# Attention scores of two heads made together, the low part of K in half the array's rows per head

## The chip, the core and the metric

The kernel runs on one core of one Trainium2 chip. The time is device microseconds (us) of one execution, from the first to the last instruction of the program with what the device needs around it. Before the change three runs took 1198.54, 1198.84 and 1199.20 us; the median is 1198.84 us.

## The reference, cut to what matters

Two layers, each with one mixer and no feed-forward. 512 latent tokens and 256 context tokens, 1024 wide. A layer normalises and modulates its input, projects it once into the queries, keys and values of three groups of heads (A, B, C, each with 8 heads of 64) and a gate, lets each group attend in its own way, multiplies by the gate, projects back and adds. The change touches group A only: global attention, 8 query heads over 2 key and value heads, so that four query heads share one K and V.

```python
def global_gqa(q, k, v, qc, kc, vc, cos, sin, qn, kn, need_ctx):
    q = apply_rope(rmsnorm(heads(q, N_HEADS_A), qn), cos, sin) * scale
    k = apply_rope(rmsnorm(heads(k, N_KV_A), kn), cos, sin)
    ...
    k_all = jnp.concatenate([k, kc], axis=1)        # 512 latent + 256 context keys
    v_all = jnp.concatenate([v, vc], axis=1)
    def block(qi):                                   # 128 queries
        s = jnp.einsum('bqhgd,bkhd->bhgqk', qi, k_all)
        p = softmax_f32(s, v_all.dtype)
        return jnp.einsum('bhgqk,bkhd->bqhgd', p, v_all)
```

## The kernel before, in words

Nearly all matmuls take operands of the type `F32R`. To keep precision each operand is split into a high part and the low rest (`hi` is x copied to `F32R`, `lo = x - hi`), and a product is made as several passes that add up in PSUM.

**Scores of group A.** A head has 64 numbers, the array 128 rows, and the kernel uses both halves. The stationary operand is a tile of Q for 128 queries: rows 0 to 63 hold the high part of q, rows 64 to 127 the low part (`a_pair`, L883 to L905, where `qd` is laid out and turned). K is held twice: `K[:, 0]` has its high part in both halves of the rows, `K[:, 1]` its low part in both halves. A pass over `K[:, 0]` so gives (q_hi + q_lo)·k_hi, and a pass over `K[:, 1]` adds (q_hi + q_lo)·k_lo. For 128 queries of one head there are four passes: 256 context keys and 512 latent keys, each over both parts of K (L1152). Every matmul in this kernel brings its own load of the stationary operand, also where the one before it used the same.

**Units.** A pair of heads is attended in units. For group A a `GlobalUnit` is one head and two tiles of 128 queries (`units`, L1308): two per head, four per pair of heads. With 4 pairs in each of 2 layers there are 32 such units. `scores()` makes the eight passes into `Sbig`, three PSUM banks of 512 numbers: tile 0 of the unit takes columns 0 to 767, tile 1 columns 768 to 1535. Then, for each tile, VectorE takes the negated maximum (`negm`, L1158) and ScalarE the exponential with its sum (`P`, L1160). `values()` turns P on TensorE (`T`, L1054), splits the turned block into `pth` (ScalarE, L798) and `ptl` (VectorE, L1044), and multiplies both with V into `Obig` (L1049). `o_out` (L1069) adds the two halves of the result: ScalarE copies 64x256 out, VectorE adds (L1072). In the first layer a `CtxUnit` per head follows for the 256 context queries. Groups B and C have units of their own, which the change leaves alone.

**Order.** The Python program writes attention and projections as generators. `weave` steps between the attention of one pair (`attend`) and the projections of a later one (`PLAN`, L33), by the costs that each `yield` names; `zipped` runs the scores of a unit beside the values of the one before. The list so written is a priority; a scheduler then puts the instructions of each engine in order, with `tc.high_priority` moving a piece ahead and `after` tying one instruction behind another on the same engine without a semaphore. The last stage of a layer projects back (`head`, `finish_result`).

**One place where the array is already cut.** The modulation vectors are made by `ada` (L203): eight matmuls with a stationary operand of two columns, in four groups of 32 columns of the array (`pm[32 * g:32 * g + 2]`, L214). They run in the 32-bit float format, where each matmul appears as two instructions, 16 in all per call.

Of the kernel before, what the change touches and what calls it, by code (L numbers as in the profile page):

```python
# [11 lines left out]
F32 = mybir.dt.float32  # L12
F32R = mybir.dt.float32r
BF16 = mybir.dt.bfloat16
AF = mybir.ActivationFunctionType
# [6 lines left out]
NT = 512  # L22
# [749 lines left out]
def mixers(tc, nc, l, last, p1, ps, const, env):  # L772
# [110 lines left out]
    def a_pair(i, bank):  # L883
# [3 lines left out]
        def done(p, t2):  # L887
# [160 lines left out]
    def mul(*args, **kw):  # L1048
        m = nc.tensor.matmul(*args, **kw)  # L1049
        pace["pe"] = m.ins.name  # L1050
        return m
# [17 lines left out]
    def o_out(O, OT, h, c0, n):  # L1069
        tmp = p1.tile([64, 512], F32, name="otmp", bufs=1)  # L1070
        nc.scalar.activation(tmp[:, 0:n], O[64:128, 0:n], AF.Copy)
        nc.vector.tensor_add(OT[64 * h:64 * h + 64, c0:c0 + n], O[0:64, 0:n], tmp[:, 0:n])  # L1072

    third = {"n": 2}

# [5 lines left out]
    class Unit:  # L1081
# [5 lines left out]

        def stat(self, name, i, n=1):
            if name not in self.c:
                self.c[name] = p1.tile([128, 12], F32, name=name, bufs=2)  # L1090
            return self.c[name][:, self.h * 6 + i:self.h * 6 + i + n]

# [51 lines left out]

    class GlobalUnit(Unit):
        def scores(self):
            self.P = []
            for i in self.tiles:
                cx, loc = ((512, 0), (768, 1024))[i % 2]
                for c0, c1, o in ((NT, NA, cx), (0, NT, loc)):  # L1150
                    for x in range(2):
                        mul(Sbig[:, o:o + c1 - c0], self.Q[:, i * 128:(i + 1) * 128],  # L1152
                                         self.K[:, x, c0:c1], start=(x == 0), stop=(x == 1), skip_group_check=True)
                yield 0.65
            for i in self.tiles:
                S = Sbig[:, 768 * (i % 2):768 * (i % 2) + 768]
                nm = self.stat("negm", i)
                nc.vector.tensor_reduce(nm, S, axis=AX.X, op=OP.max, negate=True)  # L1158
                P = newP()
                nc.scalar.activation(P, S, AF.Exp, bias=nm, accum_out=self.stat("sums", i))  # L1160
                self.P.append(P)
                yield 0

        def values(self):
            O = half_O()

            def turns(k2):
                T = psT()
                for k in range(2):
                    for j in range(2):  # L1170

                        o = ((k2 + k + 2) % 6 if j else k2 + k) * 128
                        turn(T[:, (2 * k + j) * 128:(2 * k + j + 1) * 128], self.P[j][:, o:o + 128], ident)
# [7 lines left out]
            o_out(O, self.OT(), self.h, self.tiles[0] * 128, 256)  # L1181

# [105 lines left out]
    def units(kind, i, Q, K, V, G, extra):  # L1288
        c = dict(kind=kind, i=i, Q=Q, G=G)
        out = []  # L1290
        for h in range(2):
            if kind == "B":
# [13 lines left out]
            v = lambda kb, vh=vh: V[:, kb, vh].rearrange("p x f -> p (x f)")  # L1306
            if kind == "A":
                out += [GlobalUnit(c, h, k, v, tiles=t) for t in ((0, 1), (2, 3))]  # L1308
            else:
                out.append((NearUnit if kind == "B" else BandUnit)(c, h, k, v, sink, bm))  # L1310
# [360 lines left out]
```

## Time and profile before

| | |
|---|---|
| Runs | 1198.54, 1198.84, 1199.20 us |
| Span of the profiled execution | 1197.7 us (1.1 us below the median run) |
| Busy: TensorE / weight loads / VectorE / ScalarE / GpSimd | 96% / 86% / 64% / 58% / 34% |
| Matmuls | 8016 |
| Granted TensorE clock, mean | 0.996 |
| Attention of group A within | 265 to 560 us (layer 0), 885 to 1112 us (layer 1) |

The page lists groups of instructions by line, engine and tile, with their busy time and the mean duration of one. A matmul's duration holds its way through the array and the end is modelled; what it costs a row of matmuls is the distance from its start to the next start. The timeline merges neighbours of one kind: "x8" with a start and a length, where the length runs to the end of the last one. PE is TensorE's matmuls, PEld its loads of the stationary operand, which run beside them. What follows an instruction in square brackets is the idle time of its engine ahead of it and what ended that; "issue" means that the engine waited for nothing that the profile shows.

### The profile page before, as it was taken

How to read it: one execution, taken by the hardware profiler on the slowest of the kernel's cores; microseconds unless marked ns; L12 is line 12 of the kernel's file. 1: busy time of each engine (PE TensorE's matmuls, PEld its weight loads, DVE VectorE, ACT ScalarE, POOL GpSimd, SP SyncE). 2: the span in 40 equal slices, each digit the busy share in tenths (PEclk: the TensorE clock that was granted, in tenths of full speed). 3: DMA queues.
4: the chain of work that ended last, by engine and by line, in shares of the span. 5: the costliest groups of instructions: out<-in, count | busy, mean ns of one | idle time of the engine just before them, and what ended most of it. 6: DMA issues, size and time to landing. Idle time of an engine off the chain costs nothing.

```text
span 1197.7 us, 21749 instructions
## 1 busy us (share of the span) xinstructions
PE 1150.5 (96%) x8016; PEld 1034.8 (86%) x8016; DVE 769.4 (64%) x1548; ACT 696.9 (58%) x1581; POOL 408.1 (34%) x496
## 2 busy tenths in 40 slices
PE   5999999999999999999999999999999999998997
PEld 3898999998898988988778999989988888887876
DVE  5767566764656665568578895567754556567563
ACT  5446555656666676588423544555666667677552
POOL 1341110234446354385000030202274563656001
PEclk9999999999999999999999999999999999999999
DMA  9552222313312112123086662323222111232152
GB/s 321 213 142 89 78 78 67 123 66 104 111 70 92 67 44 92 34 63 119 27 293 198 205 210 74 98 84 109 91 73 67 53 46 53 63 88 72 36 161 77
DMA packets 60826, 124.22 MB, mean 104 GB/s; under 512 B 7216, under 2 KB 13488, under 8 KB 60720
## 3 DMA queue, kind: packets, MB, share of 16 engines
q1 hardware_dynamic: 54768, 111.96, 29.6%
q10 hardware_dynamic: 5952, 10.88, 2.7%
q8 instruction: 63, 1.03, 0.3%
q14 instruction: 43, 0.35, 0.1%
HBM read 109.05 MB, written 11.14 MB: 100 GB/s over the span
## 4 chain that ended last, share of the span: by engine, by line
PE 81%; DVE 5%; ACT 5%; DMA 3%; issue 3%; POOL 1%; SPq 0%; ACTq 0%; DVEq 0%; POOLq 0%
PE pj L318 18%; PE pj L341 17%; PE Sbig L1049 9%; PE Obig L1049 9%; PE T L1054 9%; PE pj L519 5%; PE T L519 3%; PE Sbig L519 3%; PE T L341 2%; PE Sbig L430 2%; DVE ptl L1044 1%; DMA x<-xT_dram 1%; PE Sbig L341 1%; ACT pth L798 1%; PE pj L430 1%
## 5 line engine op out<-in xcount | busy, mean ns | idle before, releaser
L1044 DVE TENSOR_TENSOR ptl<-T,pth 128x512 fp32r<-128x512 f32 (+2 forms) x312 | 181.1, 591 | 128.6 <-ACT pth L798 126.7
L798 ACT ACTIVATE pth<-T 128x512 fp32r<-128x512 f32 (+2 forms) x312 | 158.9, 520 | 134.8 <-PE T L1054 128.1
L341 PE MATMUL pj<-wh,hL 128*128 128x256 f32 x896 | 180.6, 287 | 0.0
L318 PE MATMUL pj<-hL,wh 128*128 128x512 f32 x544 | 175.0, 401 | 0.9 <-ACT wh L247 0.5
L1054 PE MATMUL T<-ident,P 128*128 128x128 f32 x1024 | 165.7, 273 | 4.0 <-ACT qt L902 1.7
L247 ACT ACTIVATE wh<-ws 128x512 fp32r<-128x512 f32 x192 | 119.5, 629 | 78.6 <-PE pj L318 16.3
L1049 PE MATMUL Sbig<-kt,qt 128*128 128x256 f32 (+1 forms) x864 | 156.2, 308 | 4.6 <-ACT P L1160 2.5
L250 POOL TENSOR_TENSOR wl<-ws,wh 128x512 fp32r<-128x512 f32 x76 | 98.5, 1300 | 146.4 <-ACT wh L247 146.4
L341 PEld LDWEIGHTS pj<-wh,hL 128*128 128x128 f32 x896 | 144.2, 190 | 1.0 <-issue 0.2
L1049 PE MATMUL Obig<-pth,vt 128*128 128x256 f32 (+2 forms) x432 | 134.6, 321 | 4.6 <-ACT pth L798 2.0
L1054 PEld LDWEIGHTS T<-ident,P 128*128 128x128 f32 x1024 | 123.0, 140 | 17.6 <-DVE ptl L1044 2.2
L1049 PE MATMUL Obig<-ptl,vt 128*128 128x256 f32 (+2 forms) x432 | 131.4, 318 | 5.0 <-DVE ptl L1044 4.3
L1049 PEld LDWEIGHTS Sbig<-kt,qt 128*128 128x128 f32 x864 | 123.3, 189 | 13.4 <-DVE negm L1208 4.1
L341 PE MATMUL pj<-wl,hL 128*128 128x256 f32 x448 | 128.0, 286 | 0.0
L318 PEld LDWEIGHTS pj<-hL,wh 128*128 128x128 f32 x544 | 96.2, 189 | 16.7 <-ACT wh L247 0.9
L250 DVE TENSOR_TENSOR wl<-ws,wh 128x512 fp32r<-128x512 f32 x116 | 82.7, 720 | 40.4 <-ACT wh L247 31.6
L318 PE MATMUL pj<-hL,wl 128*128 128x512 f32 x272 | 107.1, 394 | 0.5 <-DVE wl L250 0.5
L1049 PEld LDWEIGHTS Obig<-pth,vt 128*128 128x128 f32 x432 | 81.6, 189 | 15.9 <-ACT pth L798 7.1
L1049 PEld LDWEIGHTS Obig<-ptl,vt 128*128 128x128 f32 x432 | 81.5, 189 | 14.7 <-DVE ptl L1044 11.3
L1445 POOL TENSOR_TENSOR bm<-wr,bm 128x192 f32<-128x192 f32 (+1 forms) x48 | 41.3, 888 | 139.6 <-DMA bm<-mskB_dram 132.4
L341 PEld LDWEIGHTS pj<-wl,hL 128*128 128x128 f32 x448 | 85.4, 191 | 0.3
L1158 DVE TENSOR_REDUCE negm<-Sbig 128x1 f32<-128x768 f32 x64 | 61.0, 953 | 29.7 <-PE Sbig L1049 15.7
(336 smaller groups left out, 2495.6 us busy)
## 6 DMA issues: line engine op xcount, KB each, us to landing
ws<-wf_dram SPq DMA_DIRECT2D x72, 256.0 KB, 3.1
ws<-wt_dram SPq DMA_DIRECT2D x72, 256.0 KB, 3.0
ada<-adaw_dram SPq DMA_DIRECT2D x32, 512.0 KB, 5.5
ws<-wo_dram SPq DMA_DIRECT2D x57, 256.0 KB, 2.8
bm<-mskB_dram SPq DMA_DIRECT2D x16, 576.0 KB, 3.7
dw<-adat_dram SPq DMA_DIRECT2D x8, 512.0 KB, 8.2
dots<-adat_dram SPq DMA_DIRECT2D x16, 256.0 KB, 4.5
u<-u ACTq DMA_DIRECT2D x9, 384.0 KB, 2.9
```

Of the source, the lines that this page charges most:

```text
L247: nc.scalar.activation(hi, src, AF.Copy)
L250: eng.tensor_sub(lo, src, hi.bitcast(F32))
L318: paced(nc.tensor.matmul(p[:, 0:n], a[:, r, :], cols(b[kt], c0, n), start=(i == 0), stop=(i == 23)), i)
L341: paced(nc.tensor.matmul(p[:, t * 256:(t + 1) * 256], tok(a[kt], t2 + t), b[:, r, :], start=(i == 0), stop=(i == 23)), i)
L430: mm = nc.tensor.matmul(out, a, b, start=begin, stop=(kt == KT - 1 and i == 2), skip_group_check=True)
L519: mm = nc.tensor.matmul(p[:, 0:n], a[:, r, :], ucols(ua[b][ft], c0, n), start=(ft == FT_ORDER[0] and i == 0), stop=(ft == FT_ORDER[-1] and ...
L798: nc.scalar.activation(out, src, AF.Copy)
L1044: i = nc.vector.tensor_sub(lo[:, 0:n], T[:, 0:n], hi[:, 0:n].bitcast(F32))
L1049: m = nc.tensor.matmul(*args, **kw)
L1054: m = nc.tensor.transpose(*args, **kw)
L1158: nc.vector.tensor_reduce(nm, S, axis=AX.X, op=OP.max, negate=True)
L1445: nc.gpsimd.tensor_add(b, src, b)
```

## The change

Three things are changed, all in group A.

1. **Unit.** A unit is now one tile of 128 queries and both heads of the pair (`tiles=(t,)`, four units per pair, as many as before). Head 0 has columns 0 to 767 of `Sbig`, head 1 columns 768 to 1535. The two context units of a pair come after its four global ones.
2. **Layout of Q.** Head 0 keeps high, low; head 1 is laid out low, high. The high part of head 0 is in rows 0 to 63, that of head 1 in rows 64 to 127.
3. **Passes.** Five whole passes as before: the high part of K for context and latent keys of both heads, and the low part for the context keys of head 0. The rest of the low part is done in five passes of 64 rows and 256 keys each: head 0 on rows 0 to 63, head 1 on rows 64 to 127, in turn, head 1 first. Their stationary operand is the high part of q alone, so q_lo·k_lo is no longer added there. Two neighbours in this row have different rows and different PSUM banks. The five are tied one behind the other and behind the whole passes, and raised in priority.

`o_both` takes the place of `o_out`: one copy of 64x256 on ScalarE as before, but two additions of 64x128 on VectorE, since the two heads go to different rows of `OT`. Copies and subtractions of Q are as many as before, with other strides.

```diff
-            nc.scalar.activation(qd[:, :, 0:64], t1, AF.Copy)
-            e.tensor_sub(qd[:, :, 64:128], t1, qd[:, :, 0:64].bitcast(F32))
+            blocks = qd.rearrange("p a f -> p (a f)").rearrange("p (t b f) -> p t b f", t=2, b=4)
+            hi, lo = blocks[:, :, 0:4:3], blocks[:, :, 1:3]
+            src = t1.rearrange("p (t h) f -> p t h f", t=2)
+            nc.scalar.activation(hi, src, AF.Copy)
+            e.tensor_sub(lo, src, hi.bitcast(F32))
...
+    def o_both(O, OT, c0):
+        tmp = p1.tile([64, 512], F32, name="otmp", bufs=1)
+        nc.scalar.activation(tmp[:, 0:256], O[64:128, 0:256], AF.Copy)
+        for h in range(2):
+            nc.vector.tensor_add(OT[64 * h:64 * h + 64, c0:c0 + 128], O[0:64, h * 128:h * 128 + 128],
+                                 tmp[:, h * 128:h * 128 + 128])
...
         def scores(self):
-            for i in self.tiles:
-                cx, loc = ((512, 0), (768, 1024))[i % 2]
-                for c0, c1, o in ((NT, NA, cx), (0, NT, loc)):
-                    for x in range(2):
-                        mul(Sbig[:, o:o + c1 - c0], self.Q[:, i * 128:(i + 1) * 128],
-                                         self.K[:, x, c0:c1], start=(x == 0), stop=(x == 1), skip_group_check=True)
-                yield 0.65
+            i = self.tiles[0]
+            Q = [q[:, i * 128:(i + 1) * 128] for q in self.c["Q"]]
+            whole = []
+            for h, x, c0, c1, o in ((0, 0, NT, NA, 512), (0, 1, NT, NA, 512), (1, 0, NT, NA, 768), (0, 0, 0, NT, 0),
+                                    (1, 0, 0, NT, 1024)):
+                whole.append(mul(Sbig[:, o:o + c1 - c0], Q[h], self.K[:, x, c0:c1], start=(x == 0 and o != 768),
+                                 stop=False, skip_group_check=True))
+                if o == 768:
+                    after(whole[2], whole[0].ins.name)
+                yield (c1 - c0) / 2400
+            last = None
+            for h, c0, o in ((1, NT, 768), (0, 0, 0), (1, 0, 1024), (0, 256, 256), (1, 256, 1280)):
+                r = slice(64 * h, 64 * h + 64)
+                with tc.high_priority(offset=200):
+                    m = mul(Sbig[:, o:o + 256], Q[h][r], self.K[r, 1, c0:c0 + 256], start=False, stop=True,
+                            skip_group_check=True)
+                for w in whole[1:] if last is None else (last,):
+                    after(m, w.ins.name)
+                last = m
+            yield 0.33
...
+        if kind == "A":
+            out += [GlobalUnit(c, 0, K[i // 2], v, tiles=(t,)) for t in range(4)]
...
-            if kind == "A":
-                out += [GlobalUnit(c, h, k, v, tiles=t) for t in ((0, 1), (2, 3))]
```

What this does to the order on TensorE, at the first unit of group A in layer 1. `Sbig` is written by the passes of the scores, `pj` by projections, `T` by turned blocks; L1049 of before is L1052 of the change. Before:

```order
3807 L899 MATMUL T<-identr,qd 128x128 x4
3808 L1049 MATMUL Obig<-pth,vt 128x2x128
3809 L1049 MATMUL Sbig<-kt,qt 128x256 x2
3810 L1049 MATMUL Sbig<-kt,qt 128x512 x2
3811 L1049 MATMUL Sbig<-kt,qt 128x256 x2
3812 L1049 MATMUL Sbig<-kt,qt 128x512 x2
3813 L318 MATMUL pj<-hC,wh 128x256 x2
```

The same place in the changed kernel:

```order
3804 L902 MATMUL T<-identr,qd 128x128 x4
3805 L1052 MATMUL Obig<-pth,vt 128x2x128
3806 L1052 MATMUL Sbig<-kt,qt 128x256 x3
3807 L1052 MATMUL Sbig<-kt,qt 128x512 x2
3808 L1052 MATMUL Sbig<-kt,qt 128x256 x5
3809 L318 MATMUL pj<-hL,wh 128x512 x2
```

Eight passes (four of 256 columns, four of 512) became three of 256, two of 512 and the five half-row passes, which stand in one row; this is so at all 32 units. Before, both passes of a score were neighbours and tile 0 was complete after half of the row; now the last pass of head 0 is the last but one of ten.

On VectorE, in the first pair of group A in layer 0, before (L1044 is `ptl`, L1158 the maximum, L1072 the addition of `o_out`, L1121 the maximum of a context unit):

```order
392 L1121 TENSOR_REDUCE negm<-Sbig 128x2
393 L1044 TENSOR_TENSOR ptl<-T,pth 128x512 x3
394 L1072 TENSOR_TENSOR OT<-Obig,otmp 64x256
395 L1158 TENSOR_REDUCE negm<-Sbig 128x1
396 L1044 TENSOR_TENSOR ptl<-T,pth 128x512
397 L1158 TENSOR_REDUCE negm<-Sbig 128x1
398 L1044 TENSOR_TENSOR ptl<-T,pth 128x512
399 L874 TENSOR_TENSOR vt<-T,vt 128x4x64 x2
400 L1072 TENSOR_TENSOR OT<-Obig,otmp 64x256
```

And in the changed kernel (L1047, L1185, L1082 and L1133 in the same roles):

```order
392 L1185 TENSOR_REDUCE negm<-Sbig 128x1
393 L1047 TENSOR_TENSOR ptl<-T,pth 128x512 x3
394 L1185 TENSOR_REDUCE negm<-Sbig 128x1
395 L1082 TENSOR_TENSOR OT<-Obig,otmp 64x128 x2
396 L1047 TENSOR_TENSOR ptl<-T,pth 128x512
397 L1185 TENSOR_REDUCE negm<-Sbig 128x1
398 L1047 TENSOR_TENSOR ptl<-T,pth 128x512
399 L874 TENSOR_TENSOR vt<-T,vt 128x4x64 x2
400 L1082 TENSOR_TENSOR OT<-Obig,otmp 64x128 x2
401 L1133 TENSOR_REDUCE negm<-Sbig 128x2
```

The addition is two instructions, and the context unit's maximum has moved behind the global units; the rest stands as it did.

More of the change, by code (lines that the diff above doesn't have):

```diff
@@ L1169, in turns @@
                 for k in range(2):
-                    for j in range(2):
-                        o = ((k2 + k + 2) % 6 if j else k2 + k) * 128
-                        turn(T[:, (2 * k + j) * 128:(2 * k + j + 1) * 128], self.P[j][:, o:o + 128], ident)
+                    for h in range(2):
+                        o = ((k2 + k + 2) % 6 if h else k2 + k) * 128
+                        turn(T[:, (2 * k + h) * 128:(2 * k + h + 1) * 128], self.P[h][:, o:o + 128], ident)
                 return pt_copy(T, 512)
@@ L1180, in values @@
             yield from ahead([(lambda k2=k2: turns(k2), lambda pt, k2=k2: sums(k2, pt), 0.45) for k2 in range(0, 6, 2)])
-            o_out(O, self.OT(), self.h, self.tiles[0] * 128, 256)
+            o_both(O, self.OT(), self.tiles[0] * 128)
     KS = [(0, 1), (0, 1, 2), (1, 2, 3), (2, 3)]
```

16 lines of the change are left out of this document (9 added, 7 removed).

## The prediction, made before the result was known

> **What bounds the kernel now.** I read the page first, then the timeline of TensorE (PE) and of its weight loads (PEld) around one unit of group A, then the one place where the array is already used in parts. The page's busy times, its chain and four of its groups:
>
> ```profile
> PE 1150.5 (96%) x8016; PEld 1034.8 (86%) x8016; DVE 769.4 (64%) x1548; ACT 696.9 (58%) x1581; POOL 408.1 (34%) x496
> PE 81%; DVE 5%; ACT 5%; DMA 3%; issue 3%; POOL 1%; SPq 0%; ACTq 0%; DVEq 0%; POOLq 0%
> L1054 PE MATMUL T<-ident,P 128*128 128x128 f32 x1024 | 165.7, 273 | 4.0 <-ACT qt L902 1.7
> L1049 PE MATMUL Sbig<-kt,qt 128*128 128x256 f32 (+1 forms) x864 | 156.2, 308 | 4.6 <-ACT P L1160 2.5
> L1158 DVE TENSOR_REDUCE negm<-Sbig 128x1 f32<-128x768 f32 x64 | 61.0, 953 | 29.7 <-PE Sbig L1049 15.7
> ```
>
> PE is busy for 96% of the span and makes 81% of the chain. The windows of group A (layer 0, then layer 1) show the same within the stages that the change touches:
>
> ```profile
> 265.00:560.00 295.00, 288.51 (x2130) 260.01 (x2129) 184.61 (x358) 195.19 (x453) 156.48 (x176) 1.00 0.25 80
> 885.00:1112.00 227.00, 216.23 (x1434) 191.50 (x1433) 136.29 (x247) 157.60 (x342) 126.05 (x139) 1.00 0.20 61
> ```
>
> The columns are length, then busy time of PE, PEld, VectorE (DVE), ScalarE and GpSimd. PE has 295.00 - 288.51 = 6.5 us idle in the first and 10.8 us in the second, at a full clock. So PE's time counts nearly one for one: what a unit gains or loses on PE, 32 times over, is the change in the end.
>
> **What a unit costs on PE now.** The eight passes of one unit, with the passes before and behind them:
>
> ```profile
> 385.64 0.40 PE L318 MATMUL pj<-hL,wl 128*128 128x512 f32 x1
> 385.87 1.56 PE L1049 MATMUL Sbig<-kt,qt 128*128 128x256 f32 x8
> 387.28 0.60 PE L1054 MATMUL T<-ident,P 128*128 128x128 f32 x4
> ```
>
> From 385.87 to 387.28 is 1.41 us for four passes of 256 columns and four of 512. A pass of 512 takes 385.87 - 385.64 = 0.23 from start to start; that leaves (1.41 - 4 x 0.23) / 4 = 0.12 for a pass of 256. The weight loads of these passes cost nothing of their own, since each runs under the pass before it:
>
> ```profile
> 385.64 1.36 PEld L1049 LDWEIGHTS Sbig<-kt,qt 128*128 128x128 f32 x8
> ```
>
> **What the change does to it.** Five whole passes stay: 3 x 0.12 + 2 x 0.23 = 0.82. One of 256 and two of 512 go, 0.12 + 2 x 0.23 = 0.58, and five passes of 64 rows and 256 keys take their place. If two of these run at a time they need three rounds, 3 x 0.12 = 0.36, provided nothing is lost at the border between whole and half passes. So 0.58 is the price to beat, and two questions decide: what the border costs, and whether the loads of two halves run together.
>
> **The border.** No row of before has a pass of 64 rows. The nearest thing is L214, where four matmuls share the array by columns. Its surroundings:
>
> ```profile
> 406.38 0.28 PE L341 MATMUL pj<-wl,hL 128*128 128x256 f32 x1
> 406.50 0.28 PE L341 MATMUL pj<-wh,hL 128*128 128x256 f32 x1
> 406.71 1.04 PE L214 MATMUL pj<-ada,silu_c 128*2 128x256 f32 x16
> 407.69 0.38 PE L1049 MATMUL Obig<-pth,vt 128*128 128x256 f32 x1
> 407.91 0.28 PE L1049 MATMUL Obig<-ptl,vt 128*128 128x256 f32 x1
> 408.03 0.28 PE L1049 MATMUL Obig<-pth,vt 128*128 128x256 f32 x1
> 408.26 0.60 PE L1054 MATMUL T<-ident,P 128*128 128x128 f32 x4
> L214 PE MATMUL pj<-ada,silu_c 128*2 128x256 f32 x128 | 8.4, 378 | 0.0
> ```
>
> Side by side works there: 16 passes last from 406.71 to the last start, 406.71 + 1.04 - 0.38 = 407.37, which is three rounds of four at 0.22 each. But the border has a price on both sides. Going in, the pass ahead (406.50) is followed after 0.21 instead of 0.12: 0.09 lost. Ordinary neighbours, 407.91 and 408.03, are 0.12 apart. Coming out, 407.69 - 407.37 = 0.32 instead of the 0.22 of a round: 0.10 lost. Then the first whole pass is followed after 407.91 - 407.69 = 0.22 instead of 0.12: its weight load had no pass to hide under, 0.10 lost. The loads tell that nothing else was waited for:
>
> ```profile
> 279.09 0.54 PEld L214 LDWEIGHTS pj<-ada,silu_c 128*2 128x2 f32 x16 [0.25 <-issue]
> 280.06 0.19 PEld L1049 LDWEIGHTS Obig<-pth,vt 128*128 128x128 f32 x1 [0.44 <-issue]
> ...
> 488.14 0.19 PEld L1049 LDWEIGHTS Obig<-pth,vt 128*128 128x128 f32 x1 [0.44 <-issue]
> ```
>
> All three idle times end by "issue", and behind two blocks 200 us apart it is the same 0.44. I read this as the array running empty when the way it is cut changes, with the next load held until then. The Trainium skill says the same on the page "TensorEngine Tiling (Array Packing)", section "Tiling Modes", under its key properties: a change of the tiling mode, not of the tile, drains TensorE; the trace agrees, with 0.09 going in and 0.10 coming out, and the page gives no price.
>
> For half passes one more term comes in. The loads of L214 have two columns; those of the change have 128. A load of 128 columns takes 0.11: the four turned blocks at 408.26 are bound by theirs, and start (0.60 - 0.27) / 3 = 0.11 apart, with 0.273 as the length of one from the page. Behind a drained array the first of them is bare. The skill's page "TensorE: Matmul & The Clock Gate", section "LDWEIGHTS (loading the stationary operand)", says that a load's time goes by its columns, not its rows, by which half the rows save nothing; its figure, 128 / 1.2, is an estimate of 107 ns and agrees with the 0.11.
>
> **The sum for one unit, as I forecast it.** In 0.09, first load 0.11, three rounds 0.36, out 0.10, first whole load 0.10: 0.76. Against 0.58 that is +0.18 us. The ends are 0.36 (no border at all, below zero by 0.22) and 1.00 (loads one at a time: five rounds instead of three, +0.24 on 0.76). I take 0.76 because L214 is the only row in which the array is cut, and it shows both a price and side by side. 32 units x 0.18 = +5.8 us.
>
> No semaphore is added: the half passes follow the whole ones by their place in PE's queue, and what is queued behind them (projections, mostly) waits for the 0.18 and nothing else.
>
> **The rest of the change.**
>
> ```profile
> L1072 DVE TENSOR_TENSOR OT<-Obig,otmp 64x256 f32<-64x256 f32 x56 | 23.2, 414 | 23.9 <-ACT otmp L1071 23.4
> L1072 DVE TENSOR_TENSOR OT<-Obig,otmp 64x512 f32<-64x512 f32 x32 | 21.8, 682 | 12.9 <-ACT otmp L1071 12.4
> PE Obig L1049 <- DVE OT L1072: 0.3, 1, 0.3
> PE Obig L1049 <- DVE OT L1072: 1.3, 2, 0.7
> PE Sbig L1049 <- ACT P L1160: 1.8, 2, 1.1
> PE Sbig L1049 <- ACT P L1160: 0.7, 1, 0.7
> ```
>
> (The last four are waits of PE in the two windows: us in total, times, longest; the first and third are of layer 1.)
>
> `o_both`: 682 - 414 = 268 ns for 256 columns more, so 128 columns cost about 414 - 134 = 280 ns, two of them 560 against 414: +0.15 us of VectorE per unit, 4.7 in all. VectorE is busy 184.61 of 295 and 136.29 of 227, which hides it, except where PE waits for `OT`, three times in the two windows: at most 3 x 0.15 = 0.5 us. I take 0.3. Behind the second addition stand `ptl` subtractions on VectorE, and PE behind those; that is within the same bound.
>
> The maximum of head 0 can start only when its last half pass is done, after all but one pass, where tile 0 used to be complete after 0.70. VectorE waited for scores 15.7 us in total; but PE waited for the exponentials only 1.8 + 0.7 = 2.5 us in the two windows. Between 0 and about that sum again, 2.5; I take 0, since one unit's scores run beside the values of the one before. Later context units, the stride of Q and smaller steps in the weave: 0, hidden by ScalarE and GpSimd at half load. The new order moves PE's 17.3 us of idle about in either direction; I allow 2 us.
>
> The span is 1197.7 in the profiled execution and the runs' median 1198.84; I keep the 1.1 between them. 1198.84 + 5.8 + 0.3 = 1204.9.
>
> **Rivals.**
>
> *Slower by more: loads one at a time.* If the two halves' loads share one path, each half pass waits for its own 0.11, and five follow each other at 0.12 as ordinary passes do. 1.00 a unit, +0.42 x 32 = +13.4: 1212.5. For it: the turned blocks, bound by loads that never overlap. Against it: their loads go to the same rows, and nothing shows two parts. It decides as soon as a load takes as long as a half pass streams, and 0.11 against 0.12 is nearly that.
>
> *Faster: no border for rows.* L214 cuts the columns, where each part needs its moving data led in separately; a cut by rows may not need an empty array. Then the five cost 0.36, -0.22 x 32 = -7.0, and 1198.84 - 7.0 + 0.3 = 1192.1. The switch decides: below 0.22 a unit the change gains. For it: half passes have the same 128 columns and the same output rows as whole ones. Against it: the only border in the trace. The page "TensorE: Matmul & The Clock Gate", section "Measured speedup vs the span model", speaks for this rival: it adds about 4 ns per tile packed by rows, and names no price for coming or going; no run here shows it.
>
> *The change does not do what it says.* No border and no side by side: five passes at 0.12 are 0.60 against 0.58, +0.02 x 32 = +0.6, with 0.3 more 1199.7. Or the loads hide while the array drains, leaving 0.19 + 0.36 = 0.55: -0.03 x 32 = -1.0 and 1198.1. Either is no change.
>
> **How the numbers follow.** Forecast (border as at L214, loads together) 0.32; loads one at a time 0.20; no border 0.31; neither, or a hidden load, 0.17. The forecast's own range is 1202.9 to 1209.4: 2 us of order either way, and above it the 2.5 of late exponentials. For 8 in 10 the range must reach both rivals: 1191.0 to 1212.0, which leaves out about half of "one at a time" and a third of "no border". A measurement can tell about 0.2%, 2.4 us. Slower: 0.32 less a little, and 0.20, and the upper edge of the last: 0.51. Same: most of the last, a little of the forecast: 0.16. Faster: no border and the last's lower edge: 0.33.
>
> **What would show it.** The five half passes as a group of their own with 64 rows: starts in pairs, few ns apart, 0.12 per pair (together), or 0.12 each (one at a time). From the last whole pass to the first half pass 0.21 or more (border) or 0.12. Behind the fifth, a load with idle time ended by "issue", and the next whole pass followed after 0.22. If the whole row of ten passes takes 1.58 I am right, at 1.18 the faster rival, at 1.82 the slower. I am wrong if the row takes no longer than the 1.41 of before, or if the time lies elsewhere, in waits of PE for `P`, `OT` or `ptl`.

## The result and the profile after it

The changed kernel takes 1220.74 us (median of four runs, 1217.98 to 1221.24) against 1199.02 us of the kernel before beside it (1198.54 to 1199.83). The ratio is 1.0171, with a 95% interval of 1.0156 to 1.0186: 20.5 us slower by the ratio. The forecast was 1204.9 and its range ended at 1212.0. The direction was right, the size was off by a factor of more than three, and, as the runs below show, most of the loss came from another place than the forecast's.

The page of the changed kernel, with the rows that answer to those shown of before:

```profile
span 1218.9 us, 21946 instructions
PE 1162.4 (95%) x8080; PEld 1034.4 (85%) x8080; DVE 776.4 (64%) x1580; ACT 694.3 (57%) x1581; POOL 406.8 (33%) x496
...
PE 32%; ACT 3%; DVE 3%; issue 2%; POOL 1%; DMA 0%; ACTq 0%; DVEq 0%; POOLq 0%
```

Of 1218.9 - 1197.7 = 21.2 us of span, TensorE's busy time takes 1162.4 - 1150.5 = 11.9, its idle time the other 9.3 (56.5 against 47.2). The chain adds up to 41% only, so the walk back broke off, and nothing is read from it.

**The half passes did what the forecast said.** TensorE at one unit of group A in layer 0. The first row is the whole group; the others are cut from it by narrow windows, which is why one instruction can stand in two rows:

```profile
364.35 1.54 PE L1052 MATMUL Sbig<-kt,qt 128*128 128x256 f32 x10
364.94 0.71 PE L1052 MATMUL Sbig<-kt,qt 128*128 128x512 f32 x3
365.26 0.39 PE L1052 MATMUL Sbig<-kt,qt 64*128 64x256 f32 x2
365.49 0.39 PE L1052 MATMUL Sbig<-kt,qt 64*128 64x256 f32 x3
365.61 0.28 PE L1052 MATMUL Sbig<-kt,qt 64*128 64x256 f32 x1
365.81 0.51 PE L318 MATMUL pj<-hC,wh 128*128 128x256 f32 x2
```

The weight loads of the same passes:

```profile
364.23 0.67 PEld L1052 LDWEIGHTS Sbig<-kt,qt 128*128 128x128 f32 x5
365.26 0.19 PEld L1052 LDWEIGHTS Sbig<-kt,qt 64*128 64x128 f32 x2 [0.36 <-issue]
365.37 0.19 PEld L1052 LDWEIGHTS Sbig<-kt,qt 64*128 64x128 f32 x2
365.49 0.19 PEld L1052 LDWEIGHTS Sbig<-kt,qt 64*128 64x128 f32 x1
365.81 0.30 PEld L318 LDWEIGHTS pj<-hC,wh 128*128 128x128 f32 x2
```

The last whole pass starts at 364.94 (the second row, which merges it with the first two half passes), the first half pass at 365.26: 0.32 where 0.23 is the rule, so 0.09 lost going in. The loads stand still meanwhile, 0.36 us that end by "issue". Then they come in pairs: two at 365.26, two at 365.37, one at 365.49, so the loads of two halves do run together. The half passes start at 365.26 (two), 365.49 (two) and 365.61: the first round carries its bare load, 0.23, the next 0.12. Out of the last one 365.81 - 365.61 = 0.20, 0.08 more than a round, and the first whole pass is followed after 0.51 - 0.28 = 0.23 (the pair's length less that of a pass of 256) instead of 0.12, its load bare as well. Over all 32 units of the trace the medians are 326 ns in, 341 ns from the first half pass to the last, 205 ns out, and the whole pass behind is followed 0.10 later than usual: 0.097 + 0.341 + 0.205 + 0.105 = 0.75 us for one unit, where 0.76 was forecast. That is (0.75 - 0.58) x 32 = 5.4 us.

**So some 15 us lie elsewhere.** The windows of group A, which have shifted and widened (columns as before):

```profile
265.00:573.00 308.00, 296.24 (x2181) 262.65 (x2179) 186.73 (x381) 196.00 (x455) 157.74 (x181) 0.99 0.24 76
900.00:1133.00 233.00, 221.11 (x1467) 190.94 (x1466) 139.61 (x262) 156.79 (x344) 124.25 (x139) 0.99 0.19 60
```

Layer 0 takes 13 us longer than its 295, layer 1 6 us longer than its 227; 16 units at 0.17 us account for 2.7 in each. A part of the 13 us is only work that has moved: the first window holds 2181 - 2130 = 51 matmuls more, 32 of them added by the change; the other 19 belong elsewhere and, at 0.12 to 0.23 us each, come to 2 to 4 us (an estimate). TensorE's idle time is 308.00 - 296.24 = 11.8 us in the first (6.5 before) and 11.9 in the second (10.8 before). What TensorE waits for, over the whole run, in the changed kernel (us, times, longest; L1187, L1057, L905 and L1075 have the roles of L1160, L1054, L902 and L1072 of before):

```profile
PE Obig L1052 <- DVE ptl L1047: 6.7, 14, 0.7
PE Obig L1052 <- ACT pth L798: 4.2, 7, 1.5
PE Obig L1052 <- DVE OT L1075: 3.9, 4, 2.2
PE Sbig L1052 <- ACT P L1187: 3.0, 7, 0.6
PE T L1057 <- ACT qt L905: 2.7, 3, 1.5
```

and before:

```profile
PE Obig L1049 <- DVE ptl L1044: 4.3, 11, 0.8
PE Sbig L1049 <- ACT P L1160: 2.5, 3, 1.1
PE Obig L1049 <- ACT pth L798: 2.0, 6, 0.5
PE Obig L1049 <- DVE OT L1072: 1.9, 4, 0.7
...
PE T L1054 <- ACT qt L902: 1.7, 2, 1.2
```

No one wait has taken over. Each of the five is longer, by 0.5 to 2.4 us, and they belong to different steps of the work. That is how a less fitting order looks, but not which part of the change made it.

**A small part is the clock.** The third column from the end in the windows above is TensorE's granted clock; it is 0.99 in both, where it was 1.00. Between 30 us and the last 10 us of its span the kernel before has one stretch of 3.4 us at half clock, the changed kernel two (at 543.89 and 1113.92) and the kernel with small steps, further down, three:

```profile
625.17:628.59 3.42, 3.42 (x8) 2.75 (x9) 3.42 (x6) 1.26 (x2) 0.00 (x0) 0.50 1.02 367
908.62:912.04 3.42, 3.42 (x17) 3.13 (x15) 0.85 (x2) 1.44 (x4) 0.35 (x1) 0.50 0.23 77
1024.68:1028.09 3.41, 3.41 (x16) 3.05 (x15) 2.14 (x5) 2.20 (x5) 2.80 (x4) 0.50 0.24 77
1110.01:1113.42 3.41, 2.94 (x11) 2.17 (x9) 2.87 (x4) 2.74 (x5) 2.50 (x2) 0.50 0.00 0
```

(The first is of before, the others are of the kernel with small steps.) In the first of them passes of 512 columns start 0.43 us apart (at 626.54 and 626.97, for one), where 0.23 is the rule. By that such a stretch costs 1.5 to 1.7 us, half of TensorE's busy time in it (an estimate); one more of them is 1.5 of the change's 20.5 us. Five of these six stretches begin within 3 us behind a wait of TensorE of more than 1 us, the one at 1024.68 does not, and most such waits are followed by none; what sets the stretches off was not tried.

### The profile page after: what moved, and what is told of

It reads as the page before. It is cut to its first block, busy times and chain, and to the rows that moved or that the text cites. A ratio compares the mean times of both kernels' runs of the same rounds, so it can differ in the third digit from the quotient of the medians.

```text
span 1218.9 us, 21946 instructions
## 1 busy us (share of the span) xinstructions
PE 1162.4 (95%) x8080; PEld 1034.4 (85%) x8080; DVE 776.4 (64%) x1580; ACT 694.3 (57%) x1581; POOL 406.8 (33%) x496
## 5 line engine op out<-in xcount | busy, mean ns | idle before, releaser
L1047 DVE TENSOR_TENSOR ptl<-T,pth 128x512 fp32r<-128x512 f32 (+2 forms) x312 | 182.4, 592 | 124.7 <-ACT pth L798 122.4
L1057 PE MATMUL T<-ident,P 128*128 128x128 f32 x1024 | 166.7, 275 | 1.5 <-ACT P L1238 0.5
L1052 PE MATMUL Sbig<-kt,qt 128*128 128x256 f32 (+4 forms) x928 | 154.3, 305 | 3.9 <-ACT P L1187 3.0
L1052 PE MATMUL Obig<-pth,vt 128*128 128x256 f32 (+2 forms) x432 | 137.2, 326 | 9.4 <-ACT pth L798 4.2
L1052 PE MATMUL Obig<-ptl,vt 128*128 128x256 f32 (+2 forms) x432 | 132.9, 321 | 7.1 <-DVE ptl L1047 6.7
L1052 PEld LDWEIGHTS Sbig<-kt,qt 128*128 128x128 f32 (+1 forms) x928 | 121.4, 189 | 21.3 <-issue 11.6
L1057 PEld LDWEIGHTS T<-ident,P 128*128 128x128 f32 x1024 | 123.8, 141 | 13.2 <-ACT P L1238 1.0
L1052 PEld LDWEIGHTS Obig<-pth,vt 128*128 128x128 f32 x432 | 82.4, 191 | 22.4 <-ACT pth L798 14.6
L1052 PEld LDWEIGHTS Obig<-ptl,vt 128*128 128x128 f32 x432 | 82.4, 191 | 17.8 <-DVE ptl L1047 13.6
L1185 DVE TENSOR_REDUCE negm<-Sbig 128x1 f32<-128x768 f32 x64 | 61.2, 956 | 35.4 <-ACT P L1187 17.7
```

Of the source, the lines that this page charges most:

```text
L1047: i = nc.vector.tensor_sub(lo[:, 0:n], T[:, 0:n], hi[:, 0:n].bitcast(F32))
L1057: m = nc.tensor.transpose(*args, **kw)
```

## The experiments

The ratio is always to the kernel before, run on the same chip in the same group; the bracket is its 95% interval. The theories are named by letters in what was expected:

- **P**: the half passes cost what their rows show, about 5 us, and the rest is the new order.
- **Q**: the border upsets the order, and costs far more than its rows show.
- **R**: the scores are complete too late, since the low passes come last.
- **S**: the context units at the end of a pair are in the wrong place.
- **T**: the second addition on VectorE.
- **U**: the finer steps, since `scores()` now yields after every whole pass and the weave steps between attention and projections at every `yield` (as `zipped` does between the scores of one unit and the values of another). U1: through the ties between projections and attention matmuls, which go by the last matmul made with `mul`. U2: through the order of the list, which is the scheduler's priority on every engine.
- **V**: the lower sum of the steps' costs (1.077 for a unit, against 1.3).

### Is it the half passes?

**Five whole passes in the changed kernel.** Nothing else moves; the order on every engine is that of the change.

```
-                r = slice(64 * h, 64 * h + 64)
+                r = slice(0, 128)
```

> The changed kernel with its five half passes given all 128 rows, nothing else: the order on every engine is that of the change, row by row, but the array is never cut for the scores (and q_lo times k_lo is added there again). Theory P, the half passes cost what their rows in the trace show (0.76 us with their border against 0.60 for five whole passes of 256, 0.16 a unit, 5 us in all) and the other 16 of the 21.7 us come from the new order of units: about 1215.6. Theory Q, the border is what upsets everything, because the order on the other engines was laid out for a TensorE without it, so that a small delay sets off waits: 1200 to 1204.

Measured: 1.0137 [1.0114, 1.0160], 1218.01 us against 1201.53. Without any border the kernel is still 1.37% slower, so Q falls: the half passes cost 1.0171 - 1.0137 = 0.34%, 4 us, and the intervals of the two overlap a little. P stands, and the larger part of the loss has nothing to do with what the change is named after.

**One half pass in the kernel before.** For the second tile of a unit the low pass over the context keys is made with 64 rows, in the old order.

```
+                        r = slice(0, 64) if x == 1 and c0 == NT and i % 2 else slice(0, 128)
-                        mul(Sbig[:, o:o + c1 - c0], self.Q[:, i * 128:(i + 1) * 128],
-                                         self.K[:, x, c0:c1], start=(x == 0), stop=(x == 1), skip_group_check=True)
+                        mul(Sbig[:, o:o + c1 - c0], self.Q[r, i * 128:(i + 1) * 128],
+                                         self.K[r, x, c0:c1], start=(x == 0), stop=(x == 1), skip_group_check=True)
```

> The kernel before with one pass of each unit (low part of K, context keys, second tile) on 64 rows, alone, so that every unit crosses the border in and out once and nothing runs side by side; order on every engine as before; q_lo times k_lo is left out in that pass. Price by the rows of the trace 0.10 in, 0.11 bare load, 0.09 out, 0.11 bare load, 0.41 a unit, 13 us in all. Theory P: 1212, plus or minus 2. Theory Q: the waits it sets off add as much again or more, 1225 and up.

Measured: 1.0089 [1.0069, 1.0108], 1212.17 us. 0.89% of 1201.53 is 10.7 us or 0.33 us for each of 32 crossings. A place in this kernel where a product of values stands behind the half pass:

```profile
267.18 0.50 PE L1049 MATMUL Obig<-pth,vt 128*128 128x512 f32 x1
267.51 0.63 PE L1049 MATMUL Sbig<-kt,qt 128*128 128x512 f32 x2
```

The product is followed after 267.51 - 267.18 = 0.33 where 0.23 is the rule: the bare load of the first whole pass, 0.10. With 0.09 going in, 0.11 for the half pass's own load and 0.09 coming out, one crossing costs 0.39 by such rows; 0.33 of it came out at the end. A border is paid at nearly its face value and sets nothing else off, which speaks against Q a second time.

### Is it the units?

**The new units with the old passes and steps.** `scores()` makes for each head the four passes of before, `yield 0.65` each; the units, `o_both`, the layout of Q and the place of the context units are those of the change.

```
-                yield (c1 - c0) / 2400
...
+            for h, cx, loc in ((0, 512, 0), (1, 768, 1024)):
+                for c0, c1, o in ((NT, NA, cx), (0, NT, loc)):
+                    for x in range(2):
+                        mul(Sbig[:, o:o + c1 - c0], Q[h], self.K[:, x, c0:c1], start=(x == 0), stop=(x == 1),
...
+                yield 0.65
```

> The changed kernel's units (one tile, both heads, context units last, two additions) and its layout of Q, but the passes as before the change: four whole passes per head, each score's two passes neighbours. Theory P: the units themselves cost most of the 16 us, 1210 to 1216. Theory Q: units cost nothing, 1197 to 1202.

Measured: 1.0056 [1.0036, 1.0076]. Part of the loss, a third, and between the two answers.

**The context units back between the heads' units**, everything else as in the change.

```
-            out += [GlobalUnit(c, 0, K[i // 2], v, tiles=(t,)) for t in range(4)]
+            glob = [GlobalUnit(c, 0, K[i // 2], v, tiles=(t,)) for t in range(4)]
...
+            if kind == "A":
+                out += glob[2 * h:2 * h + 2]
```

> The changed kernel with the context units back between the global ones (two global, one context, two global, one context), half passes kept. Theory P in the form that the bunched global units of layer 0 starve TensorE: some 10 us come back, about 1210. Theory Q: no change, 1219 to 1222.

Measured: 1.0213 [1.0195, 1.0232], 1227.58 us: slower than the change itself. No theory had said that. It is the first sign that the parts of this change don't add up.

**The same two together**: old passes and steps, context units between.

> The changed kernel's units with the old order of passes, all whole, and the context units back between the global ones. Theory S: the units alone lose their 7 us, 1199 to 1203. Theory R and T, or that the shape of the unit costs: 1206 to 1211, and with the context units between even more, as with the half passes, up to 1214.

Measured: 1.0004 [0.9993, 1.0015], 1200.96 us against 1200.18. The units of two heads, the stride of Q and the second addition cost nothing that can be measured. Beside the kernel above with context units last (1.0056), moving them is worth half a per cent here.

**Only the context units last, in the kernel before.**

```
+        if kind == "A":
+            out = [x for x in out if x.tiles] + [x for x in out if not x.tiles]
```

> The kernel before with only the two context units of a group A pair moved behind its four global units. Theory S, this bunching is what the units alone cost in layer 0: 1204 to 1208. Theory R and T: 1199 to 1202.

Measured: 1.0041 [1.0026, 1.0056], 1205.63 us. S is right for 5 us in this setting.

**Only the addition in two, in the kernel before.**

```
-            o_out(O, self.OT(), self.h, self.tiles[0] * 128, 256)
...
+            for t in (0, 128):
+                nc.vector.tensor_add(OT[64 * h:64 * h + 64, c0 + t:c0 + t + 128], O[0:64, t:t + 128], tmp[:, t:t + 128])
```

> The kernel before with the addition of each global unit made in two halves of 64x128 on VectorE, nothing else. Theory T, the second addition holds up the values of the next unit: 1203 to 1207. Theory R and S, and the prediction: at most 0.5 us, 1199 to 1202.

Measured: 1.0007 [0.9993, 1.0020], 1200.43 us. T falls. In the changed kernel the 64 additions take, by shape:

```profile
L1082 DVE TENSOR_TENSOR OT<-Obig,otmp 64x128 f32<-64x128 f32 x64 | 18.0, 282 | 19.5 <-ACT otmp L1080 18.8
```

282 ns each, where 280 was worked out.

### Late scores, or small steps?

**The kernel before with the change's order of passes**: the five whole ones with their `yield` after each, then three whole passes over the low part.

```
+                yield (c1 - c0) / 2400
+            for h, c0, n, o in ((1, NT, 256, 768), (0, 0, 512, 0), (1, 0, 512, 1024)):
+                mul(Sbig[:, o:o + n], Q[h], self.K[:, 1, c0:c0 + n], start=False, stop=True, skip_group_check=True)
+            yield 0.55
```

> The kernel before, units and context units as they were, whole passes only, but the passes of a unit in the order of the change: all high parts (and the low part of the first tile's context keys) first, the low parts of both tiles last. Theory R, the time goes because both scores of a unit are complete only at its end, so that maximum, exponential and turned blocks come later: 1206 to 1211, about the 9 us between the five whole passes and the units alone. Theory S (order of units) and theory T (the second addition): 1199 to 1202.

Measured: 1.0087 [1.0065, 1.0109], 1210.58 us. It looked like R. But the edit changes two things, the order of the passes and the number of steps, and the next two part them.

**Old passes in the old order, but a step after each.**

```
-                yield 0.65
+                        yield (c1 - c0) / 2400
```

> The kernel before with its old order of passes, but each pass of a unit a step of its own in the weave instead of four at a time, with the same weight in all. Theory R (scores complete late): 1199 to 1202. Theory U, what the low passes last cost came from the finer steps, which let the scheduler cut units up: 1206 to 1211.

Measured: 1.0133 [1.0113, 1.0153], 1217.62 us against 1201.34: 16 us from a line that adds no work to any engine, and more than U had expected (1206 to 1211). The kernel with the low passes last, which has five such steps and a larger one, lost less (1.0087).

**Late scores in the old steps**: the last pass of the first tile moves to the end of the unit, two steps of 0.65 as before.

```
+                        if i % 2 == 0 and x == 1 and o == loc:
+                            late = a
+                            continue
...
+                if i % 2:
+                    after(mul(*late, start=False, stop=True, skip_group_check=True), m.ins.name)
```

> The kernel before with one pass moved: the last pass of a unit's first tile (low part of K, 512 latent keys) stands behind the second tile's passes, so that the first tile is complete at 1.40 us of the row instead of 0.70 and the second at 1.17 instead of 1.40; same steps, same passes. Theory R: as much as with all low passes last or more, 1207 to 1215. Theory U: 1199 to 1202.

Measured: 1.0002 [0.9989, 1.0015], 1200.65 us. R falls, in the old steps at least, and U stands. The page of the kernel with small steps alone:

```profile
span 1216.7 us, 21756 instructions
PE 1156.3 (95%) x8016; PEld 1038.4 (85%) x8016; DVE 773.8 (64%) x1548; ACT 697.7 (57%) x1581; POOL 407.1 (33%) x496
```

As many passes as before, but 1216.7 - 1156.3 = 60.4 us of idle TensorE instead of 47.2. Of the 5.8 us more of busy time some 3.2 are its two more stretches at half clock ((3.42 + 3.41 + 2.94 - 3.42) / 2 by the rows shown above, an estimate); the rest may be short waits that the modelled ends of the matmuls cover, which is not shown. Its waits:

```profile
PE Obig L1049 <- DVE ptl L1044: 6.7, 11, 1.5
PE T L1054 <- ACT qt L902: 4.1, 4, 1.7
PE Obig L1049 <- ACT pth L798: 4.0, 8, 1.0
PE Obig L1049 <- DVE OT L1072: 4.0, 4, 1.9
```

These are nearly the changed kernel's rows again (`qt` 4.1 against 2.7), in a kernel that shares nothing with it but the steps. One of the waits can be followed in all three kernels: the copy of Q (`qt`) for the next pair, late in group A of layer 0. ScalarE before:

```profile
522.37 0.90 ACT L1160 ACTIVATE P<-Sbig,negm 128x768 f32<-128x768 f32 x1
...
523.82 0.59 ACT L1071 ACTIVATE otmp<-Obig 64x512 f32<-64x512 f32 x1
525.39 0.66 ACT L902 ACTIVATE qt<-T 128x256 fp32r<-128x256 f32 x2 [0.97 <-PE T L899]
...
526.41 0.91 ACT L1160 ACTIVATE P<-Sbig,negm 128x768 f32<-128x768 f32 x1
```

With small steps only:

```profile
533.43 0.63 ACT L491 ACTIVATE hL<-uf 128x512 fp32r<-128x512 f32 x1 [1.58 <-PE pj L318]
534.09 0.59 ACT L1071 ACTIVATE otmp<-Obig 64x512 f32<-64x512 f32 x1
534.71 0.90 ACT L1160 ACTIVATE P<-Sbig,negm 128x768 f32<-128x768 f32 x1
...
535.60 0.65 ACT L902 ACTIVATE qt<-T 128x256 fp32r<-128x256 f32 x2
```

and TensorE there:

```profile
533.70 0.46 PE L899 MATMUL T<-identr,qd 128*128 128x128 f32 x4
...
536.30 0.66 PE L1054 MATMUL T<-ident,tR 128*128 128x128 f32 x4 [1.68 <-ACT qt L902]
```

The same place in the changed kernel, ScalarE and TensorE:

```profile
532.86 0.63 ACT L491 ACTIVATE hL<-uf 128x512 fp32r<-128x512 f32 x1 [1.75 <-PE pj L318]
...
534.28 0.62 ACT L491 ACTIVATE hL<-uf 128x512 fp32r<-128x512 f32 x1
534.92 0.59 ACT L1074 ACTIVATE otmp<-Obig 64x512 f32<-64x512 f32 x1
535.53 0.66 ACT L905 ACTIVATE qt<-T 128x256 fp32r<-128x256 f32 x2
536.25 0.66 PE L1057 MATMUL T<-ident,tR 128*128 128x128 f32 x4 [1.50 <-ACT qt L905]
```

Before, `qt` comes as soon as TensorE has turned its blocks; `otmp` is done by then, and the next exponential `P` comes only behind `qt`. With small steps the blocks are turned at 533.70 + 0.46 = 534.16, but `qt` starts at 535.60, 1.4 us later: `otmp` is still running and the exponential now stands ahead, 0.59 and 0.90 us of work. TensorE stands for 1.68. In the changed kernel it is a copy `hL` and `otmp` that stand ahead, 0.62 and 0.59. The wait of `hL` in the first row of either is at most a small part of it, since it ends 0.7 us and more before the blocks are turned. ScalarE is busy for only 57% of the run; here several pieces of its work fall due close together, and the one that TensorE needs comes last. This is one place of several; that the rest of the loss is made of such places was not followed one by one.

**The change with the sum of costs of before**: every `yield` of the passes by the same factor.

```
-                yield (c1 - c0) / 2400
+                yield (c1 - c0) / 2400 * 1.3 / 1.077
...
-            yield 0.33
+            yield 0.33 * 1.3 / 1.077
```

> The changed kernel with the steps of a unit weighted to the 1.30 of before instead of 1.08, nothing else. Theory R: 1219 to 1222, no change. Theory V, that attention runs ahead of the projections because its steps weigh less: 1205 to 1214.

Measured: 1.0174 [1.0157, 1.0192], 1222.85 us. V falls: with the sum of before the time is that of the change.

**Half passes first, context units between, small steps.** The five half passes come first, then the whole ones of head 0 and of head 1, so that head 0 is complete early. The context units move as in the edit further up.

```
+                    m = mul(Sbig[:, o:o + 256], Q[h][r], self.K[r, 1, c0:c0 + 256], start=(o in (768, 0, 1024)),
+                            stop=False, skip_group_check=True)
...
+            yield 0.33
+            for h, x, c0, c1, o in ((0, 0, NT, NA, 512), (0, 1, NT, NA, 512), (0, 0, 0, NT, 0), (1, 0, NT, NA, 768),
+                                    (1, 0, 0, NT, 1024)):
...
+                yield (c1 - c0) / 2400
```

> The changed kernel with its five half passes at the head of the unit instead of its end, then head 0 whole, then head 1, and the context units between the global ones. Head 0 is complete 0.35 us ahead of the end of the row instead of 0.12. Theory R: part of the 9 us comes back and the context units' 5 too, 1206 to 1212; the half passes keep their 4 us. If only the half passes and the context units mattered: 1203. If neither: 1219 or more, as with the context units between before.

Measured: 1.0206 [1.0191, 1.0221], 1225.91 us: a miss for the hope of a better version, and next to the 1.0213 above, which has the same steps and units with the half passes last.

### Two steps in the changed kernel

```
-                yield (c1 - c0) / 2400
+            yield 0.65
...
-            yield 0.33
+            yield 0.65
```

One step after the five whole passes, one after the half passes; context units last, as in the change.

> The changed kernel in two steps, context units last as the change has them. Theory U with 5 us for the context units: 1208 to 1211. If the fine steps are what made the place of the context units matter: 1203 to 1206.

Measured: 1.0052 [1.0033, 1.0071], 1207.90 us, between the two answers. **With context units between** in addition:

> The changed kernel with its half passes, but its scores in two steps of the weave (five whole passes, 0.65; five half passes, 0.65) as the unit before had, and the context units back between the global ones. Theory U (steps and place of the context units cost all but the half passes' own 0.16 a unit): 1203 to 1206. If the half passes had a share beyond their own rows in the trace: 1208 and up.

Measured: 1.0033 [1.0021, 1.0044], 1205.44 us. The row of busy times on its page:

```profile
PE 1158.3 (96%) x8080; PEld 1033.1 (86%) x8080; DVE 774.6 (64%) x1580; ACT 695.9 (58%) x1581; POOL 408.9 (34%) x496
```

The span is 1204.8, so TensorE is idle for 46.5 us, no more than the 47.2 before. Its longest waits:

```profile
PE Obig L1052 <- DVE ptl L1047: 4.9, 14, 0.7
PE Obig L1052 <- ACT pth L798: 2.5, 7, 0.7
PE Obig L1052 <- DVE OT L1075: 2.0, 4, 1.1
...
PE T L1057 <- ACT qt L905: 1.6, 2, 1.2
```

They are back near those of before. One of its units on TensorE, from its first pass at 373.81 to the next instruction at 375.27, takes 1.46 us, the same as in the change (365.81 - 364.35).

**The same with five whole passes** (`r = slice(0, 128)`), with an order equal to that of the kernel above on every engine; q_lo·k_lo is added again.

> The same kernel, the same order on every engine, with all 128 rows in the five half passes (q_lo times k_lo added there again): 5 x 0.12 instead of 0.76 with its border. Theory U: 4 to 5 us below the run with half passes, 1199 to 1201.5. No theory expects it below 1198.

Measured: 1.0006 [0.9997, 1.0016], 1202.78 us. This is the cleanest price of the half passes: 1.0033 - 1.0006 = 0.27%, 3.2 us. The rows of one unit make (0.75 - 0.60) x 32 = 4.8 us against five whole passes of 256, so two thirds of it arrive at the end, less than the 4 to 5 us expected.

**Which way do small steps act?** The kernel with small steps alone, but only the last pass of a tile moves the point to which projections are tied:

```
-                        mul(Sbig[:, o:o + c1 - c0], self.Q[:, i * 128:(i + 1) * 128],
+                        (mul if x == 1 and c0 == 0 else nc.tensor.matmul)(Sbig[:, o:o + c1 - c0], self.Q[:, i * 128:(i + 1) * 128],
```

> The kernel before in the small steps that cost 1.33%, old order of passes, but only the last pass of a tile is offered as the point that a projection matmul may be tied behind. Theory U1, fine steps hurt because the projections are tied behind the attention more tightly: back to 1199 to 1203. Theory U2, they hurt because passes, copies and projections are listed in finer turn, so that the scheduler orders the in-order queues of ScalarE and VectorE otherwise: 1211 to 1219.

Measured: 1.0085 [1.0065, 1.0105], 1211.79 us, well above U1's answer and inside U2's. In this kernel the ties (U1) account for 1.33 - 0.85 = 0.5%; the rest is put down to the order of the list (U2), which no run changed by itself.

**Are fewer steps better still?** One `yield 1.3` for a unit, in the kernel before:

```
-                yield 0.65
+            yield 1.3
```

> The kernel before with the eight passes of a unit as one step of the weave instead of two. If steps go one way, coarser is better and this beats the kernel before: 1193 to 1197. If two steps were a good choice and the effect is that of any other listing: 1200 to 1206.

Measured: 1.0000 [0.9990, 1.0010], 1200.84 us. And in the changed kernel with context units between, one `yield 1.3` behind all ten passes:

> The changed kernel with its half passes, context units between, all ten passes as one step. If coarser is better: below the 1205 of two steps by 2 to 5 us, 1200 to 1203, still not below the kernel before by more than its 3 us for the border allow. If not: 1204 to 1210.

Measured: 1.0090 [1.0077, 1.0103], 1212.15 us, above both answers, where two steps gave 1.0033. There is no rule "the coarser the better". No version here beats the kernel before.

## Why the prediction was wrong, step by step

A path through these kernels from before to the change, one part at a time:

| Step | Ratio after it | Step's share |
|---|---|---|
| New units, stride of Q, two additions, context units between | 1.0004 [0.9993, 1.0015] | 0 |
| Order of passes of the change, five whole, two steps | 1.0006 [0.9997, 1.0016] | 0 |
| Half passes for the whole ones | 1.0033 [1.0021, 1.0044] | 0.27%, 3 us |
| Context units last | 1.0052 [1.0033, 1.0071] | 0.2%, 2 us, intervals overlap |
| A step after every whole pass (the change; with the old sum of costs 1.0174) | 1.0171 [1.0156, 1.0186] | 1.2%, 14 us |

- **The failed step** is the sentence "Later context units, the stride of Q and smaller steps in the weave: 0, hidden by ScalarE and GpSimd at half load." The stride is 0. The small steps are 14 us on this path and 16 us alone. Context units last are 2 us on this path and 5 us alone; with small steps the sign turns (1.0213 with them between, 1.0171 with them last). The reason given was wrong in kind: a share of busy time over the whole run says nothing about one place, where `qt` stood behind 0.59 and 0.90 us of other work of a ScalarE that is at 57%. The list of what is changed, ahead of the prediction, names three things; the `yield` after every whole pass, which stands in the diff below that list, is a fourth, and it costs the most.
- "The new order moves PE's 17.3 us of idle about in either direction; I allow 2 us" was too narrow by the same error. TensorE's idle time rose by 9.3 us, by 13.2 with small steps alone, and the stretches at half clock come on top (some 1.5 and 3.2 us).
- **The half passes**: right in each term. In 0.09 forecast, 0.10 measured; first load 0.11, 0.11; rounds 0.12, 0.12; out 0.10, 0.09; first whole load 0.10, 0.10; together 0.76 and 0.75. A row of ten passes with the bare load behind it was to take 1.58 and takes 1.46 + 0.10 = 1.56, the prediction's own sign of being right. At the end 3 to 4 us arrived, measured against five whole passes; the forecast's terms make (0.76 - 0.60) x 32 = 5.1 against these, 5.8 against the passes of before. The prediction's sign of being wrong came true as well: a good part of the rest lies in longer waits of TensorE (for `ptl` 2.4 us more, for `pth` 2.2, for `OT` 2.0). So the mechanism that was forecast gave the direction for 3 to 4 us only; that the other 16 or so had the same sign was luck.
- **The second addition**: 0.3 us forecast; alone 0.07% [-0.07, 0.20]. **The late maximum of head 0**: taken as 0; late scores alone make 1.0002.
- **The rivals** were about the half passes alone, all three. Loads one at a time, no border at all, and a row that costs no more than before (0.55 to 0.60) are refuted by the rows of the loads and by the 0.75. None of them was about the order, though the listings ahead of the prediction show the passes and a context unit moved.

What stays open: which positions in which queue make up the whole of the 14 us, and how ties and list order share it in the changed kernel itself. The parts are not additive (small steps 1.33% and context units last 0.41% alone; together with units and five whole passes 1.37%), so a share belongs to its path. Nor is it shown that fine steps as such are at fault: one step for ten passes costs too (1.0090 against 1.0033 with two), one step for eight does not (1.0000). The runs show that the order which comes out of the list costs time; none of these times was foreseen from the list.

## What to carry to other kernels

When an edit touches code that a weave or a scheduler cuts into steps, treat the number and the place of its `yield`s as a change of its own: take the edit apart, and run the new work in the old steps and the old work in the new steps. Here the work cost 3 us and the steps 14.

A half-array group pays for its border once per crossing, in and out, 0.39 us here, and then two half passes take the time of one; by these rows (an estimate, not tried) ten half passes of two units in one group would take 0.39 + 5 x 0.12 = 0.99 us for 2 x 0.58 = 1.16 us of whole passes, while five alone lose.

An engine at half load can still hold up the one that bounds the kernel: here ScalarE, busy for 57%, and TensorE idle for 1.68 us at one place. Look at what stands ahead of the instruction that the bound engine waits for.

## What the runs showed of the hardware

- A cut by rows has the same border as the cut by columns at L214: 0.10 going in and 0.09 coming out, against 0.09 and 0.10. The Trainium skill's page "TensorEngine Tiling (Array Packing)", section "Tiling Modes", says under its key properties that a change of mode drains TensorE; the traces agree in so far as about 0.1 us is lost on either side, for rows as for columns.
- Loads of 128 columns into the two halves run together (two at 365.26, two at 365.37), so a pair of half passes costs one round of 0.12. The Trainium skill's page "TensorE: Matmul & The Clock Gate", section "Measured speedup vs the span model", adds some 4 ns for each packed tile; inside a group the trace agrees, since two half passes start within the 0.01 us that the rows resolve. The 0.39 of a crossing is not in that model.
